# Rotary embedding moved from VectorE to GpSimd, in place in SBUF, with ScalarE copying whole heads out of PSUM

## The chip, the cores and the metric

The kernel runs on one core of one Trainium2 chip. The core has five engines that work side by side, each through its own list of instructions in order: TensorE (PE in the profile, with PEld for its weight loads), VectorE (DVE), ScalarE (ACT), GpSimd (POOL) and SyncE (SP), which issues most DMA transfers. The metric is the device time of one execution in microseconds; less is better. Runs of the kernel before took 1145.68, 1145.86 and 1147.49 us, the median is 1145.86 us.

## The reference: what is computed

The program is a trunk of two layers on 512 tokens of width 1024, each a token mixer and a squared-ReLU MLP with a layer norm behind each. The first mixer is sparse attention, and only that one uses the rotary embedding:

```python
def partial_rotary(t, cos, sin):
    half = cos.shape[-1]                       # 8; a head has 64 columns
    t1 = t[..., :half]; t2 = t[..., half:2 * half]
    return jnp.concatenate([t1 * c - t2 * s, t2 * c + t1 * s, t[..., 2 * half:]], axis=-1)

def dsa_mixer(x, cos, sin, w_in, w_o):
    q, k, v, iq, ik, iw = jnp.split(x @ w_in, A_SPLITS, axis=-1)
    q, k, iq, ik = (partial_rotary(z, cos, sin) for z in (q, k, iq, ik))
    # an indexer (iq, ik, iw) scores each causal key, the best 128 are kept,
    # softmax attention of 16 query heads over 4 key heads on the kept keys
```

Only the first 16 of a head's 64 columns are rotated; the other 48 pass through.

## The kernel before

Every matrix product is done in three passes (`mm3`, lines 197 to 199): both operands are split into a high part (`w_hi`, `XT` plane 0) and a low part (`w_lo`, `XT` plane 1). ScalarE casts the high part of a weight panel (L141), VectorE subtracts for the low part (L142). For the tokens `to_xt` transposes a tile of 128 tokens on TensorE (L242); ScalarE casts the high part of the result into `XT` (L244), VectorE subtracts the low part (L245). `XT` is what all products of the layer read, so a tile of tokens can start when its `XT` is there. `natural` computes one tile of 128 tokens times up to 512 columns into a PSUM bank `ps`, of which there are three.

Attention goes through five column panels of the input projection: 264 and 320 columns for the indexer (`iq`, `ik`), 512 for keys and values, twice 512 for the queries. In the first panel the tokens' tiles come in the order 1, 2, 3, 0, and `to_xt` of the next tile is done in the middle of a tile. Behind each tile stands `rotated` (19 tiles in all: 8 of 8 heads, 3 of 5, 7 of 4, 1 of one head), and behind that `stack_q` or `stack_k`: ScalarE casts the rotated tile `nat` into `hl` (L577) or `dup` (L595), VectorE subtracts for the low half (L578, L596; for `dup` ScalarE casts once more, L597), and one or two tiles later TensorE transposes it (L585, L605) and ScalarE copies the result away (L586, L607).

Meanwhile VectorE does other work. `index_scores` has TensorE compute scores (L631, L632, two PSUM banks `qk`), ScalarE apply relu (L634) and VectorE add them up (L636, L638). `top_k` then takes the 128 best of each row in rounds of MAX8 and MATCH_REPLACE8 (L679, L680), 16 rounds for each of three blocks, all on VectorE. Then the logits (L702, L703, again in `qk`), whose row extreme VectorE takes (L704), ScalarE's Exp (L708, L710), transposes (L717) and the product with the values.

GpSimd does nothing in attention. It first works in the MLP behind it, on weight combinations (L163 to L171), and later in the gated linear attention of layer two (L935, L1107).

A scheduler fixes the order of each engine's instructions when the program is built, from its own estimates and from the priorities of the code's order; on the chip each engine goes through its list in that order, and waits where an operand isn't ready.

Of the kernel before, what the change touches and what calls it, by code (L numbers as in the profile page):

```python
# [20 lines left out]
OP = mybir.AluOpType  # L21
# [84 lines left out]
class Trunk:  # L106
# [450 lines left out]
    def rotated(self, src, t, h):  # L557

        nc = self.nc
        src = src.rearrange("p (h d) -> p h d", d=64)  # L560
        dst = self.rt.tile([P, self.rt_h, 64], F32, name="nat")[:, :h, :]
        c = self.cos[:, t, None, None, :].to_broadcast([P, h, 2, 8])
        s = self.sin[:, :, t].rearrange("p two e -> p () two e").to_broadcast([P, h, 2, 8])
        x2 = src[:, :, 0:16].rearrange("p h (two e) -> p h two e", two=2)
        nc.scalar.copy(dst[:, :, 16:64], src[:, :, 16:64])
        a = self.rt.tile([P, self.rt_h, 2, 8], F32, name="rot_c")
        b = self.rt.tile([P, self.rt_h, 2, 8], F32, name="rot_s")
        nc.vector.tensor_tensor(a[:, :h], x2, c, op=OP.mult)
        nc.vector.tensor_tensor(b[:, :h], x2[:, :, ::-1, :], s, op=OP.mult)
        nc.vector.tensor_add(dst[:, :, 0:16].rearrange("p h (two e) -> p h two e", two=2), a[:, :h], b[:, :h])  # L570
        return dst

    def stack_q(self, nat, h, dst):
# [663 lines left out]
```

## Time and profile before

| | us |
|---|---|
| runs | 1145.68, 1145.86, 1147.49 |
| median | 1145.86 |
| profiled execution, its own time | 1145.4 |
| its span, first to last instruction | 1143.6 |
| busy: TensorE, VectorE, ScalarE, GpSimd | 1126.0, 883.2, 563.7, 212.9 |
| stretch with `rotated` in it | 12 to 135 |

The span lies inside the execution's time, 1.8 us less. Busy time of TensorE includes the modelled end of pipelined matmuls, so that small waits don't show in it; the idle time by stretch and the list of waits do.

### The profile page before, as it was taken

Reading aid. Unit: us, or ns where it says so; the run is one execution under the profiler, and the core shown is the slowest. Engines: PE = TensorE matmul, PEld = TensorE weight load, DVE = VectorE, ACT = ScalarE, POOL = GpSimd, SP = SyncE. Lnnn points to the kernel's source line nnn. Section 1 sums busy time; section 2 is a strip of 40 time slices with the busy share of each in tenths; the row PEclk is TensorE's granted clock in tenths of the full one; section 3 lists DMA queues with packets and bytes.
Section 4 is the critical chain, followed back from the end, with each engine's and each line's share of the span. In section 5 each row is a group of like instructions: output and inputs, shape, how many; then the busy total and the mean of one; then the engine's idle time right before and its main releaser. Section 6 shows DMA issues by size and latency. Waiting matters only on the chain. (4 is left out here: it accounts for less than half of the span.)

```text
span 1143.6 us, 16057 instructions
## 1 busy us (share of the span) xinstructions
PE 1126.0 (98%) x6039; PEld 943.5 (82%) x6039; DVE 883.2 (77%) x1592; ACT 563.7 (49%) x973; POOL 212.9 (19%) x136
## 2 busy tenths in 40 slices
PE   9999999999999999999999999999999999999997
PEld 7887888888888888888797887888988888888875
DVE  7899997687976786786885387567696876786787
ACT  6655786543544444353356476435344444343342
POOL 0000000002123213203301255110042123213221
PEclk9999999999999999999999999999999999999999
DMA  7322130521421431441432232052222421431321
GB/s 252 98 74 75 37 112 1 154 88 38 147 84 64 148 112 47 137 142 55 112 109 77 63 112 90 23 148 74 83 91 86 148 92 56 147 117 52 127 74 74
DMA packets 58198, 109.12 MB, mean 95 GB/s; under 512 B 5205, under 2 KB 10841, under 8 KB 58121
## 3 DMA queue, kind: packets, MB, share of 16 engines
q1 hardware_dynamic: 56968, 103.91, 28.7%
q0 software_dynamic: 1152, 4.19, 1.3%
q8 instruction: 47, 0.77, 0.3%
q14 instruction: 31, 0.25, 0.1%
HBM read 105.99 MB, written 2.10 MB: 95 GB/s over the span
## 5 line engine op out<-in xcount | busy, mean ns | idle before, releaser
L142 DVE TENSOR_TENSOR w_lo<-raw,w_hi 128x1024 fp32r<-128x1024 f32 (+4 forms) x220 | 288.9, 1331 | 29.1 <-ACT w_hi L141 26.7
L141 ACT CAST w_hi<-raw 128x1024 fp32r<-128x1024 f32 (+4 forms) x220 | 223.6, 1024 | 120.6 <-PE ps L199 45.8
L197 PE MATMUL ps<-XT,w_hi 128*128 128x512 f32 (+1 forms) x640 | 236.0, 369 | 0.0
L198 PE MATMUL ps<-XT,w_hi 128*128 128x512 f32 (+1 forms) x640 | 235.5, 368 | 0.0
L199 PE MATMUL ps<-XT,w_lo 128*128 128x512 f32 (+1 forms) x640 | 235.5, 368 | 0.0
L197 PE MATMUL ps<-w_hi,XT 128*128 128x512 f32 (+5 forms) x440 | 163.7, 372 | 0.8 <-ACT w_hi L141 0.8
L198 PE MATMUL ps<-w_lo,XT 128*128 128x512 f32 (+5 forms) x440 | 160.9, 366 | 0.6 <-DVE w_lo L142 0.6
L199 PE MATMUL ps<-w_hi,XT 128*128 128x512 f32 (+5 forms) x440 | 160.3, 365 | 0.0
L198 PEld LDWEIGHTS ps<-XT,w_hi 128*128 128x128 f32 x640 | 120.7, 189 | 20.2 <-issue 0.4
L197 PEld LDWEIGHTS ps<-XT,w_hi 128*128 128x128 f32 x640 | 120.6, 189 | 20.2 <-issue 0.2
L199 PEld LDWEIGHTS ps<-XT,w_lo 128*128 128x128 f32 x640 | 120.6, 188 | 20.1 <-issue 0.2
L163 POOL TENSOR_TENSOR raw<-raw 128x1024 f32<-128x1024 f32 x14 | 34.2, 2441 | 385.4 <-DVE w_lo L142 385.4
L197 PE MATMUL ps<-w_hi,form 128*128 128x512 f32 x260 | 102.2, 393 | 0.7 <-DVE big L419 0.7
L198 PE MATMUL ps<-w_lo,form 128*128 128x512 f32 x260 | 101.4, 390 | 0.0
L199 PE MATMUL ps<-w_hi,form 128*128 128x512 f32 x260 | 101.4, 390 | 0.0
L197 PEld LDWEIGHTS ps<-w_hi,XT 128*128 128x128 f32 x440 | 82.8, 188 | 12.0 <-ACT w_hi L141 1.0
L198 PEld LDWEIGHTS ps<-w_lo,XT 128*128 128x128 f32 x440 | 82.8, 188 | 11.1 <-DVE w_lo L142 1.0
L199 PEld LDWEIGHTS ps<-w_hi,XT 128*128 128x128 f32 x440 | 82.8, 188 | 10.9
L142 DVE TENSOR_TENSOR w_lo<-t,w_hi 128x1024 fp32r<-128x1024 f32 x14 | 30.3, 2164 | 72.7 <-ACT w_hi L141 72.7
L371 DVE TENSOR_TENSOR h<-h 128x512 f32<-128x512 f32 (+1 forms) x72 | 43.7, 624 | 44.2 <-ACT h L370 44.2
L370 ACT ACTIVATE h<-ps 128x512 f32<-128x512 f32 (+1 forms) x72 | 38.7, 546 | 61.5 <-PE ps L199 54.5
L141 ACT CAST w_hi<-t 128x1024 fp32r<-128x1024 f32 x14 | 14.7, 1049 | 105.3 <-POOL t L165 105.3
(248 smaller groups left out, 1950.4 us busy)
## 6 DMA issues: line engine op xcount, KB each, us to landing
raw<-in_mlp_w_up_dram SPq DMA_DIRECT2D x64, 512.0 KB, 4.4
raw<-in_mlp_w_down_dram SPq DMA_DIRECT2D x64, 512.0 KB, 4.4
raw<-in_b_w_in_dram SPq DMA_DIRECT2D x16, 512.0 KB, 4.9
raw<-in_a_w_in_dram SPq DMA_DIRECT2D x12, 512.0 KB, 4.6
big<-in_x_dram SPq DMA_DIRECT2D x8, 512.0 KB, 4.0
raw<-in_a_w_o_dram SPq DMA_DIRECT2D x8, 512.0 KB, 4.0
raw<-in_b_w_o_dram SPq DMA_DIRECT2D x8, 512.0 KB, 4.7
raw<-in_b_w_in_dram SPq DMA_DIRECT2D x8, 346.0 KB, 3.9
```

What stands on the lines that cost most here:

```text
L141: self.nc.scalar.copy(hi, src)
L142: self.nc.vector.tensor_sub(lo, src, hi.bitcast(F32))
L163: sub(t1, b12, b11)
L197: mmul(out, lhs[0], rhs[0], start=first, stop=False, skip_group_check=more)
L198: mmul(out, lhs[0], rhs[1], start=False, stop=False, skip_group_check=more)
L199: mmul(out, lhs[1], rhs[0], start=False, stop=last, skip_group_check=more)
L370: nc.scalar.activation(h, ps[:, :step], AF.Relu)
L371: nc.vector.tensor_mul(h, h, h)
```

## The change

`rotated` copies all 64 columns of each head out of the bank, not 48, and the three instructions that rotate the first 16 columns run on GpSimd in place of VectorE. They read the copy in SBUF, where they read the bank before, and the last writes over the 16 columns it was made from. So they now start after the copy, and the bank is released by the copy alone.

```diff
-        x2 = src[:, :, 0:16].rearrange("p h (two e) -> p h two e", two=2)
-        nc.scalar.copy(dst[:, :, 16:64], src[:, :, 16:64])
+        x2 = dst[:, :, 0:16].rearrange("p h (two e) -> p h two e", two=2)
+        nc.scalar.copy(dst, src)
         a = self.rt.tile([P, self.rt_h, 2, 8], F32, name="rot_c")
         b = self.rt.tile([P, self.rt_h, 2, 8], F32, name="rot_s")
-        nc.vector.tensor_tensor(a[:, :h], x2, c, op=OP.mult)
-        nc.vector.tensor_tensor(b[:, :h], x2[:, :, ::-1, :], s, op=OP.mult)
-        nc.vector.tensor_add(dst[:, :, 0:16].rearrange("p h (two e) -> p h two e", two=2), a[:, :h], b[:, :h])
+        nc.gpsimd.tensor_tensor(a[:, :h], x2, c, op=OP.mult)
+        nc.gpsimd.tensor_tensor(b[:, :h], x2[:, :, ::-1, :], s, op=OP.mult)
+        nc.gpsimd.tensor_tensor(x2, a[:, :h], b[:, :h], op=OP.add)
         return dst
```

The scheduler then orders attention anew; behind attention the lists are the same but for one ISA instruction of GpSimd, which stood ahead of its first subtraction (L163) and now stands ahead of the first rotation (L568), as GpSimd's first instruction of the kernel's own.

ScalarE in the first panel, from the copy of the first tile on (`nat` the rotated tile, `XT` the transposed tokens of the next). Before:

```order
L565 COPY nat<-ps 128x4x48
L577 CAST hl<-nat 128x3x64
L595 CAST dup<-nat 128x128
L244 CAST XT<-tps 128x4x128
L597 CAST dup<-dup 128x64
L244 CAST XT<-tps 128x4x128
L141 CAST w_hi<-raw 128x2x320 x2
L565 COPY nat<-ps 128x4x48
L244 CAST XT<-tps 128x4x128
```

Now:

```order
L565 COPY nat<-ps 128x256
L577 CAST hl<-nat 128x3x64
L595 CAST dup<-nat 128x128
L597 CAST dup<-dup 128x64
L244 CAST XT<-tps 128x4x128 x2
L141 CAST w_hi<-raw 128x2x320 x2
L565 COPY nat<-ps 128x256
L577 CAST hl<-nat 128x3x64
L595 CAST dup<-nat 128x128
L597 CAST dup<-dup 128x64
L244 CAST XT<-tps 128x4x128 x2
```

The last cast of `dup`, which needs VectorE's subtraction on the rotated tile, has moved ahead of the `XT` copies. With the second tile it is the same: `hl`, both casts of `dup`, then both copies to `XT`, where before one `XT` copy came first.

ScalarE at the first logits, in the query panels (`big` holds the transposed queries, `pr` the logits). Before:

```order
L565 COPY nat<-ps 128x8x48
L586 CAST big<-tps 128x512 x2
L708 ACT_TABLE_LOAD
L708 ACTIVATE pr<-pr,mx 128x128
L577 CAST hl<-nat 128x8x64
L708 ACTIVATE pr<-pr,mx 128x128 x4
```

Now:

```order
L565 COPY nat<-ps 128x512
L586 CAST big<-tps 128x512 x2
L577 CAST hl<-nat 128x8x64
L708 ACT_TABLE_LOAD
L708 ACTIVATE pr<-pr,mx 128x128 x5
L720 COPY pT<-tps 128x512
```

The `hl` cast has moved ahead of the load of the Exp table and of the first exponential. On VectorE the subtraction of this `hl` stood behind five L704 and now stands behind two. At the index scores of block 2 the `dup` cast of the first key tile has moved in the same way, from behind the first two relu instructions to ahead of them.

VectorE in the first half of the query panel, around the subtraction for the third tile's `hl` (`m` the eight greatest values of a round of top-k, `sc` the scores). Before:

```order
L679 MAX m_1311<-sc_218 128x8
L680 MATCH_REPLACE sc_218<-m_1311,sc_218 128x384
L142 TENSOR_TENSOR w_lo<-raw,w_hi 128x1024 x2
L578 TENSOR_TENSOR hl<-nat,hl 128x8x64
L679 MAX m_1314<-sc_218 128x8
L568 TENSOR_TENSOR rot_c<-ps,cos 128x128
L569 TENSOR_TENSOR rot_s<-ps,sin 128x128
```

Now:

```order
L679 MAX m_1317<-sc_218 128x8
L679 MAX m_1602<-sc_219 128x8
L680 MATCH_REPLACE sc_218<-m_1317,sc_218 128x384
L578 TENSOR_TENSOR hl<-nat,hl 128x8x64
L682 TENSOR_SCALAR sc_218<-sc_218 128x384
L142 TENSOR_TENSOR w_lo<-raw,w_hi 128x1024
L680 MATCH_REPLACE sc_219<-m_1602,sc_219 128x512
L142 TENSOR_TENSOR w_lo<-raw,w_hi 128x1024 x2
L679 MAX m_1605<-sc_219 128x8
```

The subtraction has moved ahead of the two `w_lo`. Of the 96 top-k instructions 82 now stand ahead of the first L704, 73 before; nine stand between it and the 33rd L704 in both.

## Rows read from the trace of the kernel before

**Rows 1.** The page of the profiled execution: its span, and part 1, busy time, share of the span and instructions of each engine.

```profile
span 1143.6 us, 16057 instructions
...
PE 1126.0 (98%) x6039; PEld 943.5 (82%) x6039; DVE 883.2 (77%) x1592; ACT 563.7 (49%) x973; POOL 212.9 (19%) x136
```

**Rows 2.** Busy time by stretch (from, to and length in us; then busy us and instructions of TensorE, its weight loads, VectorE, ScalarE and GpSimd, the granted clock of TensorE as a share of full speed, the share of DMA and its GB/s). The stretches are the first two panels and the start of the third, the key and value panel with the index scores, the first half of the query panel, the first logits, the second half of the query panel and the logits of block 1, the logits of blocks 1 and 2.

```profile
12.00:45.00 33.00, 33.00 (x239) 31.11 (x239) 25.18 (x64) 23.19 (x57) 0.00 (x0) 1.00 0.62 202
...
45.00:90.00 45.00, 44.97 (x229) 35.88 (x228) 44.11 (x127) 26.98 (x53) 0.00 (x0) 1.00 0.15 48
...
90.00:105.00 15.00, 14.23 (x73) 11.65 (x72) 14.81 (x35) 8.69 (x13) 0.00 (x0) 1.00 0.44 137
...
105.00:120.00 15.00, 14.14 (x93) 11.36 (x91) 14.86 (x62) 10.37 (x23) 0.00 (x0) 1.00 0.02 5
...
120.00:150.00 30.00, 29.86 (x214) 26.56 (x212) 26.40 (x85) 22.43 (x46) 0.00 (x0) 1.00 0.23 71
...
150.00:165.00 15.00, 14.54 (x97) 12.18 (x96) 14.63 (x41) 13.68 (x39) 0.00 (x0) 1.00 0.23 71
```

**Rows 3.** Waits from 12 to 165 us: who waited for whom; us in total, times, the longest. The rows are of TensorE (PE) and its weight loads (PEld).

```profile
PE tps L585 <- ACT w_hi L141: 0.8, 1, 0.8
...
PE qk L702 <- DVE mx L704: 0.6, 2, 0.4
...
PEld qk L702 <- DVE mx L704: 2.6, 6, 0.8
...
PEld tps L717 <- DVE XT L245: 0.6, 1, 0.6
```

**Rows 4.** The views of the tiles `nat` and `rot_s` over the whole span: line, engine, operation, how often; shortest, median and longest duration in ns; first and last start; the sizes.

```profile
L565 ACT COPY nat<-ps x19: 212/360/482, 12.6 to 132.4; 128x384 f32<-128x384 f32 x8, 128x192 f32<-128x192 f32 x7, 128x240 f32<-128x240 f32 x3, 128x48 f32<-128x48 f32 x1
...
L570 DVE TENSOR_TENSOR nat<-rot_c,rot_s x19: 174/241/286, 13.4 to 133.7; 128x128 f32<-128x128 f32 x8, 128x64 f32<-128x64 f32 x7, 128x80 f32<-128x80 f32 x3, 128x16 f32<-128x16 f32 x1
...
L569 DVE TENSOR_TENSOR rot_s<-ps,sin x19: 166/230/281, 13.2 to 133.1; 128x128 f32<-128x128 f32 x8, 128x64 f32<-128x64 f32 x7, 128x80 f32<-128x80 f32 x3, 128x16 f32<-128x16 f32 x1
```

**Rows 5.** The timeline in the gated linear attention, where GpSimd subtracts (start, duration, engine, line, operation, names and sizes, in brackets idle time before and what ended it): a copy on ScalarE and the two GpSimd instructions behind it.

```profile
650.66 0.45 ACT L1096 COPY big<-ps 128x346 f32<-128x346 f32 x1 [1.92 <-PE ps L199]
...
651.26 0.61 POOL L935 TENSOR_TENSOR Q<-gb 128x256 f32<-128x256 f32 x1 [3.19 <-ACT big L1096]
...
651.84 1.04 POOL L935 TENSOR_TENSOR E<-gb 128x512 f32<-128x512 f32 x1
```

**Rows 6.** The timeline of GpSimd and VectorE where GpSimd first computes, in the first MLP, and the view of line 389 over the whole span (shortest, median, longest ns of its 14 instructions).

```profile
214.09 0.53 POOL L326 DMA_DIRECT2D lngb<-in_ln_mlp_b_dram  x1
...
270.95 2.72 POOL L163 TENSOR_TENSOR raw<-raw 128x1024 f32<-128x1024 f32 x1 [56.33 <-DVE w_lo L142]
...
271.44 2.77 DVE L389 TENSOR_TENSOR big<-big,h 128x512 f32<-128x512 f32 x1
...
L389 DVE TENSOR_TENSOR big<-big,h x14: 673/675/2774, 271.4 to 1066.2; 128x512 f32<-128x512 f32 x14
```

**Rows 7.** The timeline of the first panel, ScalarE, then VectorE, then TensorE. The TensorE rows are the first matmul of the third and of the fourth tile.

```profile
12.61 0.32 ACT L565 COPY nat<-ps 128x192 f32<-128x192 f32 x1 [0.33 <-PE ps L199]
...
13.72 0.35 ACT L577 CAST hl<-nat 128x192 fp32r<-128x192 f32 x1 [0.79 <-DVE nat L570]
...
14.52 0.59 ACT L244 CAST XT<-tps 128x512 fp32r<-128x512 f32 x1 [0.25 <-PE tps L242]
...
16.88 0.33 ACT L565 COPY nat<-ps 128x192 f32<-128x192 f32 x1
...
18.28 0.59 ACT L244 CAST XT<-tps 128x512 fp32r<-128x512 f32 x1 [1.07 <-PE tps L242]
...
16.40 1.56 DVE L142 TENSOR_TENSOR w_lo<-raw,w_hi 128x640 fp32r<-128x640 f32 x2
...
18.90 0.69 DVE L245 TENSOR_TENSOR XT<-tps,XT 128x512 fp32r<-128x512 f32 x1 [0.42 <-ACT XT L244]
...
16.20 0.28 PE L197 MATMUL ps<-w_hi,XT 128*128 128x264 f32 x1
...
20.19 0.27 PE L197 MATMUL ps<-w_hi,XT 128*128 128x64 f32 x1
```

**Rows 8.** The timeline of ScalarE at the first index scores of block 2.

```profile
45.10 0.87 ACT L634 ACTIVATE r<-qk 128x384 f32<-128x384 f32 x2 [0.54 <-PE qk L632]
...
45.86 0.62 ACT L595 CAST dup<-nat 128x512 fp32r<-128x512 f32 x1
```

**Rows 9.** The timeline of VectorE ahead of the transposes of the third query tile.

```profile
91.85 0.56 DVE L679 MAX8 m<-sc 128x8 f32<-128x384 f32 x1
...
92.98 2.35 DVE L142 TENSOR_TENSOR w_lo<-raw,w_hi 128x1024 fp32r<-128x1024 f32 x2
...
95.25 0.69 DVE L578 TENSOR_TENSOR hl<-nat,hl 128x512 fp32r<-128x512 f32 x1
```

**Rows 10.** The timeline of ScalarE at the first logits.

```profile
108.01 0.48 ACT L565 COPY nat<-ps 128x384 f32<-128x384 f32 x1 [3.61 <-PE ps L199]
...
109.49 1.28 ACT L708 ACT_TABLE_LOAD   x1
...
110.78 0.40 ACT L708 ACTIVATE pr<-pr,mx 128x128 f32<-128x128 f32 x1
```

## The prediction, made before the changed kernel had run

> **What bounds the kernel now.** I read the page first [rows 1]: TensorE counts as busy for 98% of the span, VectorE for 77%, GpSimd for 19%. A share over the whole span says little about an edit that touches 19 tiles in one layer, so I went to the stretch in which `rotated` runs, 12 to 135 us, and to what follows it in attention, up to 165 us. The table by stretch [rows 2] shows two regimes. From 12 to 45 us TensorE has no idle time and VectorE has slack (25.2 of 33 us). From 45 to 120 us VectorE is full (44.1 of 45, 14.8 of 15, 14.9 of 15 us), because the top-k instructions fill every hole, and still TensorE idles only 0.03 + 0.77 + 0.86 us there, 0.14 us in the next 30 and 0.46 us in the 15 after. So a full VectorE is not the bound: it works off a queue that TensorE mostly doesn't wait for. What TensorE and its weight loads do wait for from 12 to 165 us is in [rows 3]: 0.8 us before the transposes of `hl` (L585), 0.6 us of matmul and 2.6 us of weight-load waits on the reduce of the logits (L704), 0.6 us on the `XT` subtraction. A weight-load wait is partly hidden behind the matmul before it, so it is an upper bound of what it costs. The granted clock is at its upper level in every stretch [rows 2], so the clock is no part of the case. The profiled execution took 1145.4 us, 0.46 us under the median of the three runs, 1145.86; I sum against 1145.4 and add the 0.46 at the end.
>
> **What VectorE gives up.** 57 instructions, three for each of 19 tiles, of 0.23 to 0.24 us in the median [rows 4], some 13.5 us of durations; they overlap their neighbours by about a quarter, so about 10 us of its time. None of it is TensorE time by itself. It pays only where a wait of [rows 3] ends earlier.
>
> **What GpSimd takes on.** The same 57 instructions, which no row shows on GpSimd in these sizes. Its nearest rows are two undisturbed subtractions in SBUF with a stretched operand, 0.61 us for 256 and 1.04 us for 512 elements per partition [rows 5]: 0.0017 us per element and 0.18 us fixed, so 0.29 us for 64 and 0.40 us for 128 elements. The lower bound is the fixed part, 0.18 us, the upper one 0.61 us, which is the larger row itself; I take the line. The start after ScalarE's copy costs about 0.15 us (a copy that ends at 651.11, GpSimd at 651.26 [rows 5]). From the end of the copy to the end of the addition that makes 0.15 + 3 x 0.29 + 0.1 = 1.1 us for four heads and 1.5 us for eight. Before, with four heads and VectorE free, it was 0.8 us from copy to `hl` [rows 7]; in the full stretch VectorE needs longer than that anyway, since its rotation stands behind top-k instructions.
>
> **What ScalarE takes on.** A quarter or a third more elements in 19 copies of 0.36 us [rows 4], at most 0.1 us each; ScalarE is busy for 105 of these 153 us [rows 2], so I put it at nothing apart from the places below. The costly thing is not the copy: `hl` and `dup` are ScalarE casts that wait for the rotation, everything behind them on ScalarE waits too, and the order has moved them forward.
>
> **Loss 1, the first panel.** ScalarE now does the second `dup` cast ahead of both `XT` copies (the first place shown in the section on the change). Tile three starts at 16.20 us on `XT` halves whose copy began at 14.52 [rows 7]. Now `hl` comes 0.4 us later and the third cast stands in front: the copy begins at about 15.2, VectorE's half (0.69 us [rows 7]) ends at about 16.5, and TensorE needs it 0.24 us after 16.20: 0.2 us lost (0 to 0.6). The next hand-over is worse. The copy of 16.88 slips to about 17.4; GpSimd could start at 17.95, but VectorE's two `w_lo` subtractions (1.56 us from 16.40 [rows 7], now from about 17.1) read SBUF twice. With 1.1 us of rotation and 1.0 us of `hl`, `dup`, the subtraction for `dup` and its cast, the `XT` copy begins at 20.0 to 20.6 instead of 18.28, and its second half is there at 21.3 to 21.9; the matmuls that stood at 20.19 need it at about 20.6. I take 1.0 us (0.6 to 1.6). Nothing behind it gives it back, since TensorE has no idle time in these 33 us.
>
> **Loss 2, the index scores.** `dup` moves from behind the second relu (45.86, the relus at 45.10) to ahead of both [rows 8], and waits for a rotation that can't end before 45.2. The relus come 0.7 us later; two banks of logits cover some of it. I take 0.5 us (0 to 1.3).
>
> **Loss 3, the first logits.** `hl` moves ahead of the load of the Exp table (the second place). The copy is at 108.01, the table at 109.49, the first exponential at 110.78 [rows 10]. Now `hl` can start at 110.1 and ends at 110.7, the table takes 1.28 us, the first exponential begins at 112.0: 1.2 us later. On VectorE `hl` stands behind the second L704 and holds the third until 111.4. TensorE's new order has three more matmuls of 0.23 us ahead of the first L717, which cover some 0.7 us. I take 0.5 us (0 to 1.2).
>
> **Gain 1.** The 0.77 us at 95.2 us: the transposes wait for an `hl` subtraction that ran at 95.25, behind two `w_lo` of 2.35 us together [rows 9]. In the new order it stands ahead of both (the third place). I take all, 0.8 us.
>
> **Gain 2.** VectorE reaches the first L704 without a rotation and with nine top-k instructions fewer outstanding, but the order still mixes nine of them with the next 32 L704, as before. Of 0.6 us idle and 2.6 us of weight-load waits [rows 3] I take 0.7 us (0 to 2.6).
>
> **Gain 3.** Top-k ends some ten microseconds of VectorE work earlier and both `w_lo` for the output projection leave the stretch after 150 us, while one `w_hi` of 1.05 us enters it. Of the 0.14 + 0.46 us idle and the 0.6 us behind `XT` [rows 2, 3] I take 0.5 us (0 to 1.2).
>
> **Sum.** Losses 0.2 + 1.0 + 0.5 + 0.5 = 2.2 us, gains 0.8 + 0.7 + 0.5 = 2.0 us: +0.2 us, 1145.6 for a profiled execution, 1146.0 for the median of runs. With all lower losses and upper gains it is 0.6 - 4.6 = -4.0 us, with the reverse 4.7 - 0.8 = +3.9 us.
>
> **Who blocks whom.** Where GpSimd ran a subtraction of 2.72 us, a VectorE instruction with two SBUF inputs that takes 0.675 us lasted 2.77 us [rows 6]: one of the two waits for the whole of the other. [...] If every VectorE instruction held GpSimd, it would be rival B.
>
> **Rivals.** A, faster: VectorE is the hidden bound from 90 to 165 us. For it speaks that it is full there and that all of [rows 3] but one names VectorE or what follows it. Against it: the same density of top-k between logits. It needs gains 2 and 3 near their ends and losses near the lower ones; about -3.4 us, 1142.5. B, slower, by one mechanism: GpSimd and VectorE exclude each other whatever the VectorE instruction. Then a GpSimd instruction stands behind the rest of a top-k instruction (0.56 us in the middle size [rows 9]) each time, so a rotation of 1.5 us becomes up to 3.2 us, and VectorE is held in turn, up to 57 x 0.3 to 0.4 us, more than the 10 us it gave up: gains 2 and 3 go, loss 2 becomes 1.3 and loss 3 2.2 us, 0.2 + 1.0 + 1.3 + 2.2 - 0.8 = +3.9 us, 1149.8. For it speaks how complete the blocking of [rows 6] is, against it that those rows are all of two SBUF inputs. It decides from about 0.18 us of VectorE held per GpSimd instruction, where the 10 us are used up. C, slower: an ISA instruction now stands ahead of the first rotation (it stood ahead of L163). If it is a code load that lasts beyond 12.9 us, the first `hl` and with it the `XT` copies wait, microsecond for microsecond; 15 us too long would give 1161. The trace can't price it: between the last DMA issue at 214.09 and the first subtraction at 270.95 GpSimd waited for data anyway [rows 6], so it lies between 0 and 56 us, and since that first subtraction isn't late I take the low end. [...]
>
> **Chances.** Near-cancellation 0.51, with a range of its own of 1143.7 to 1148.2; A 0.22, B 0.21, C 0.04; 0.02 for what I don't see. A run can tell about 0.2%, 2.3 us, from no change. The middle case spills a little over both bounds: faster 0.24, the same 0.50, slower 0.26. The range takes in the ends of the sum, 1142.0 to 1150.0.
>
> **What would show it.** In the changed profile the GpSimd rotations at 0.3 to 0.4 us each; a first-panel wait of about 1 us on `XT` at 20 us; no wait before the transposes at 95 us; the Exp table about 1 us later after the copy; L702 still waiting on L704. Wrong would be rotations of over 0.6 us, VectorE's MAX8 longer beside them, or a GpSimd that starts late.

## The result: 1.3% slower, and the profile after

The changed kernel ran in 1158.18, 1159.82, 1163.35 and 1165.86 us, median 1161.59; the kernel before beside it in 1145.8. The ratio is 1.0133, 95% interval 1.0113 to 1.0152. The profiled execution is the fastest of the four; its span is 1156.2 us, 12.6 us more than before. The page's first lines, against [rows 1]:

```profile
span 1156.2 us, 16080 instructions
...
PE 1131.0 (98%) x6039; PEld 948.5 (82%) x6039; DVE 878.0 (76%) x1535; ACT 565.8 (49%) x973; POOL 239.3 (21%) x193
```

VectorE gave up 5 us of busy time and GpSimd took on 26. Busy shares can't tell where 12.6 us went. The start of ScalarE's copy out of the bank, tile by tile, can, since TensorE's product ends just ahead of it:

| copy (L565) | before, us | after, us | later by |
|---|---|---|---|
| 1st, first panel | 12.61 | 13.26 | 0.65 |
| 5th, second panel | 27.49 | 33.29 | 5.80 |
| 7th, ahead of the index scores of block 1 | 36.31 | 42.14 | 5.83 |
| 8th, third panel | 43.58 | 52.00 | 8.43 |
| 13th, second query tile | 82.35 | 92.72 | 10.38 |
| 16th, first logits follow | 101.83 | 111.27 | 9.44 |
| 18th | 126.19 | 139.09 | 12.90 |
| end of the mixer, first L370 | 252.62 | 265.26 | 12.64 |

The loss is made in four places, all in attention: 5.2 us in the first panel, 2.6 at the index scores of block 1, 2 in the key panel, 3.5 at the first logits; 0.9 is gained at 95 us. The 0.65 at the start isn't the change's: other kernels below with the same beginning stand between -0.2 and +0.8 there.

The table by stretch, with the stretches and columns of [rows 2]:

```profile
12.00:45.00 33.00, 29.86 (x203) 28.40 (x201) 15.76 (x27) 19.41 (x45) 8.15 (x21) 0.90 0.49 157
45.00:90.00 45.00, 42.66 (x213) 33.59 (x214) 41.55 (x105) 28.92 (x60) 6.22 (x15) 1.00 0.25 80
90.00:105.00 15.00, 15.00 (x78) 12.45 (x77) 14.40 (x35) 7.35 (x12) 2.69 (x6) 1.00 0.01 1
...
120.00:150.00 30.00, 26.58 (x168) 22.92 (x168) 26.81 (x91) 20.66 (x43) 3.06 (x6) 0.94 0.15 44
```

Read two columns. TensorE is idle for 3.1, 2.3 and 3.4 us in the first, second and last stretch, where before it was idle for 0.00, 0.03 and 0.14 us. (The first logits, which now begin at 118 us, lay before in the stretch from 105 to 120 us, with 0.86 us idle.) And the granted clock, third from the end, is 0.90 and 0.94 in the first and the last stretch, where it was 1.00. Cut finer, with the same columns, after:

```profile
24.00:31.00 7.00, 7.00 (x36) 7.00 (x36) 4.49 (x6) 4.87 (x11) 0.62 (x3) 0.53 0.59 179
...
120.00:127.00 7.00, 4.09 (x19) 3.39 (x19) 6.79 (x27) 3.95 (x9) 0.00 (x0) 0.76 0.00 0
```

The first of these stretches before:

```profile
24.00:31.00 7.00, 7.00 (x52) 6.99 (x51) 4.07 (x11) 3.73 (x12) 0.00 (x0) 1.00 0.89 296
```

From 24 to 31 us TensorE never pauses, and yet does 36 matmuls where the kernel before does 52: the granted clock is 0.71 in the first of these microseconds and 0.50 in the other six. That costs 7 x 0.47 = 3.3 us; from 120 us on it is 7 x 0.24 = 1.7 us. TensorE's waits from 12 to 165 us, against [rows 3]:

```profile
PE qk L702 <- DVE mx L704: 3.5, 2, 3.3
PE qk L631 <- ACT r L634: 1.9, 3, 1.3
PE tps L585 <- DVE XT L245: 1.5, 1, 1.5
PE tps L605 <- ACT dup L595: 1.1, 1, 1.1
PE qk L631 <- ACT iqT L586: 0.8, 1, 0.8
```

The wait of [rows 3] at 95 us is gone; these five are new or longer. So the profiled execution lost some 5 us to the clock and the rest to waits. The other runs had mean clocks of 0.992, 0.988 and 0.985, the profiled one 0.993: what they lost beyond it goes with the clock.

**Where each wait comes from.** The first panel, by timelines of GpSimd, ScalarE and TensorE:

```profile
18.48 0.88 POOL L568 TENSOR_TENSOR rot_c<-nat,cos 128x64 f32<-128x64 f32 x1 [3.77 <-ACT nat L565]
...
20.99 0.24 ACT L597 CAST dup<-dup 128x64 fp32r<-128x64 f32 x1 [0.36 <-DVE dup L596]
21.14 1.07 ACT L244 CAST XT<-tps 128x512 fp32r<-128x512 f32 x2
...
22.50 0.45 PE L585 MATMUL tps<-ident_r,hl 128*128 128x128 f32 x3 [1.53 <-DVE XT L245]
```

The `XT` casts stood at 18.28 [rows 7] and 19.22 before; now they stand behind the last `dup` cast, and TensorE waits 1.53 us. It waits in the transposes of `hl`: they write to a bank `tps` that the `XT` subtraction has to read first. The index scores, on GpSimd and ScalarE:

```profile
42.63 1.45 POOL L568 TENSOR_TENSOR rot_c<-nat,cos 128x80 f32<-128x80 f32 x1 [3.74 <-ACT nat L565]
...
44.86 0.46 ACT L577 CAST hl<-nat 128x320 fp32r<-128x320 f32 x1 [1.66 <-POOL nat L570]
45.22 0.65 ACT L634 ACTIVATE r<-qk 128x256 f32<-128x256 f32 x2
```

A rotation lasts 1.45 us, four times its 0.36, beside two `w_lo` subtractions; `hl` waits for it, and the relus that TensorE needs stand behind `hl`. The first logits, TensorE and VectorE:

```profile
118.50 0.27 PE L702 MATMUL qk<-kT,big 128*128 128x128 f32 x1
...
121.97 0.68 DVE L680 MATCH_REPLACE8 sc<-m,sc 128x512 f32<-128x512 f32 x1
122.56 0.28 DVE L704 CUSTOM_DVE_ANT_0 pr<-qk,cft 128x128 f32<-128x128 f32 x1
122.91 0.33 PE L702 MATMUL qk<-kT,big 128*128 128x128 f32 x1 [3.26 <-DVE mx L704]
```

The first logits were there at 118.7, but L704 stands behind the last of 82 top-k instructions, and both `qk` banks are full.

### The profile page after: what moved, and what is told of

Read it like the earlier page. It is cut to its first block, busy times and chain, and to the rows that moved or that the text cites. A ratio compares the mean times of both kernels' runs of the same rounds, so it can differ in the third digit from the quotient of the medians.

```text
span 1156.2 us, 16080 instructions
## 1 busy us (share of the span) xinstructions
PE 1131.0 (98%) x6039; PEld 948.5 (82%) x6039; DVE 878.0 (76%) x1535; ACT 565.8 (49%) x973; POOL 239.3 (21%) x193
## 3 DMA queue, kind: packets, MB, share of 16 engines
q0 software_dynamic: 1152, 4.19, 1.3%
## 5 line engine op out<-in xcount | busy, mean ns | idle before, releaser
L163 POOL TENSOR_TENSOR raw<-raw 128x1024 f32<-128x1024 f32 x14 | 34.2, 2441 | 385.5 <-DVE w_lo L142 385.5
L197 PEld LDWEIGHTS ps<-w_hi,XT 128*128 128x128 f32 x440 | 84.0, 191 | 11.7 <-ACT w_hi L141 0.8
L199 PEld LDWEIGHTS ps<-w_hi,XT 128*128 128x128 f32 x440 | 84.2, 191 | 11.1
L370 ACT ACTIVATE h<-ps 128x512 f32<-128x512 f32 (+1 forms) x72 | 38.6, 545 | 59.8 <-PE ps L199 52.8
```

What stands on the lines that cost most here:

```text
L163: sub(t1, b12, b11)
L197: mmul(out, lhs[0], rhs[0], start=first, stop=False, skip_group_check=more)
L199: mmul(out, lhs[1], rhs[0], start=False, stop=last, skip_group_check=more)
L370: nc.scalar.activation(h, ps[:, :step], AF.Relu)
```

## The experiments

Medians are compared with runs of the kernel before on the same chip, 1146.9 to 1147.6 us in the median. Those runs go from 1145.2 us, at a mean clock of 0.998, to 1149.3 us, at 0.995: the clock varies by that much without any change.

**One group of tiles at a time.** `first_vec` and `only_first` split the change at the first panel. The edit calls the old `rotated` (here `rotated_v`) at the named places; one of the lines:

```diff
-                        nat = self.rotated(ps[:, 0:256], t, 4)
+                        nat = self.rotated_v(ps[:, 0:256], t, 4)
```

> The changed kernel, but the four tiles of the first panel rotate on VectorE out of the bank as before; the other 15 tiles stay on GpSimd, and every list behind the first panel stays as in the changed kernel. Theory 'wait, then clock': the wait of 1.7 us at 20.8 us (transposes of hl behind the late XT subtraction) and the half clock from 24.4 to 31 us that follows it go together; TensorE is 5 us earlier at the third panel and the median is 5 us under the changed kernel's 1161.6, so about 1156 to 1157. Rival 'ports' (GpSimd held by two-input VectorE instructions is what costs): only one of the eight held rotations lies in the first panel (0.88 in place of 0.32 us), so 0.6 us at most is gained. Rival 'clock falls by itself': the clock falls somewhere between 20 and 45 us anyway, gain under 2 us.

> The kernel before, but the four tiles of the first panel rotate on GpSimd as in the changed kernel; the 15 others stay on VectorE. 'Wait, then clock': the whole loss of the first panel returns, a wait of 1.5 to 1.7 us near 20.8 us and a stretch of some 6 us at half clock behind it, median 1145.8 + 5 = 1151 (1149 to 1152). 'Ports': 0.6 us at most, 1146.4. 'Clock falls by itself': within 2 us of before.

Measured: `first_vec` 1154.9 us, 6.7 under the changed kernel; `only_first` 1151.3, 4.3 over before (ratio 1.0034, 1.0020 to 1.0047). The stretch behind the first panel in both, columns as above:

```profile
24.00:31.00 7.00, 7.00 (x52) 6.98 (x51) 3.32 (x7) 3.59 (x11) 1.03 (x3) 1.00 0.90 300
```
```profile
24.00:32.00 8.00, 8.00 (x38) 8.00 (x38) 4.59 (x7) 4.81 (x11) 0.62 (x3) 0.50 0.59 172
```

With the rotations of four tiles the wait of 1.5 us and the half clock come and go together. "Ports" (one rotating instruction of 0.88 us in place of 0.32) and "clock falls by itself" are out as the account of this loss: they allow 0.6 and under 2 us.

The same with the other groups:

> The kernel before, but only the three tiles of five heads (second panel, ahead of the index scores of block 1) rotate on GpSimd. In the changed kernel TensorE lost about 3 us around them, in two waits of 0.8 and 1.3 us on the casts of iqT and on relu, with a rotation of the third tile that lasted 1.45 us in place of 0.36 beside the two-input subtraction w_lo. Theory 'waits': the order brings the waits back here, 1.5 to 3 us, median 1147.5 to 1150, and up to 3.4 us more in executions in which the clock falls behind them. Rival 'heritage' (the waits in the changed kernel came only from the panel before being late, so that weight loads and rotation met): nothing is lost, 1146 to 1147.

> The kernel before, but only the four tiles of keys (4 heads, third panel) rotate on GpSimd. 'Waits': the last rotation meets a w_lo subtraction and the dup transposes wait about 1.1 us, as at 82 us of the changed kernel; median 1146.5 to 1148.5, no clock fall from one wait of 1.1 us. 'Heritage': no such wait, 1145.5 to 1147.

> The kernel before, but only the eight query tiles (8 heads) rotate on GpSimd. The wait of 0.8 us at 95 us goes (-1.0 us in the changed kernel). At the first logits 78 top-k instructions stand ahead of the first L704 on VectorE (82 in the changed kernel, 73 before). 'Order': that is what made the 3.3 us wait, so here a wait of 1 to 2.5 us and in some executions the half clock behind it: median 1146.5 to 1150. Rival 'heritage' (the wait came from everything being 9 us late): no wait, the gain at 95 us stays, 1145.

| alone on GpSimd | median | over before | ratio, interval |
|---|---|---|---|
| first panel, 4 tiles | 1151.3 | 4.3 | 1.0034 (1.0020 to 1.0047) |
| five heads, 3 tiles | 1153.8 | 6.9 | 1.0053 (1.0034 to 1.0072) |
| keys, 4 tiles | 1148.9 | 2.0 | 1.0017 (1.0008 to 1.0026) |
| queries, 8 tiles | 1153.6 | 6.7 | 1.0063 (1.0048 to 1.0077) |

Each group loses by itself, so "heritage" is out. All three came out over what I expected, `only_kv` by 0.4 us, `only_idx` by as much even with the fall of the clock that I allowed for, `only_q` by 3.6. Their waits (of `only_idx`, then of `only_q`) and clock:

```profile
PE qk L631 <- ACT r L634: 1.4, 1, 1.4
PE qk L702 <- DVE mx L704: 1.2, 1, 1.2
...
105.00:130.00 25.00, 23.70 (x121) 21.23 (x120) 20.78 (x79) 14.32 (x31) 0.00 (x0) 0.73 0.02 7
```
```profile
PE qk L702 <- DVE mx L704: 3.9, 2, 3.4
...
110.00:120.00 10.00, 6.54 (x32) 5.64 (x32) 9.31 (x33) 6.04 (x13) 1.21 (x3) 0.66 0.00 1
```

In `only_idx` no rotation near the first logits is on GpSimd, and the order there still changed enough for a wait of 1.2 us; the clock then stayed down for most of 15 us. One of its six runs, at a mean clock of 0.996 in place of 0.989 to 0.991, took 1147.98 us, the others 1153.7 to 1155.1. The four losses sum to 20 us, more than the whole change's 15.8, since two of them pay for the same fall at the first logits.

**The copy without the engine.** `inplace_vec` has the three instructions on `nc.vector`, everything else as in the change.

> The changed kernel with the three rotating instructions on VectorE, still in place on ScalarE's copy of whole heads: it separates the copy and the dependence on it from the engine. 'Wait, then clock' with the engine's latency and the order that follows from it as the cause: a rotation of about 0.7 us behind the copy in place of 1.0 to 1.1, so waits in the first panel of 0 to 0.7 us, no clock fall, 1145 to 1149. Rival 'copy' (ScalarE's whole copy and the start behind it are the cause, whatever the engine): a wait over 1.2 us near 20 us and the clock fall return, over 1150.

Measured 1149.1 us, ratio 1.0022 (1.0013 to 1.0032). The copies of the first panel stand 0.1 to 0.2 us behind before, so the whole copy and the start behind it cost next to nothing there. The list changed at the first logits again: L702 waits 1.8 us on L704, and the clock from 110 to 120 us is 0.66. So 2 of the 16 us come without GpSimd, by the order; the rest comes with the move to GpSimd, by its longer rotation or by the order that goes with it, which this run doesn't separate.

**The wait filled.** `fill14` adds, ahead of the transposes that waited:

```diff
+    if upto == 3:
+        po = self.po.tile([P, 512], F32, name="po")
+        for _ in range(14):
+            self.nc.tensor.matmul(po[:, :256], self.ident_r, self.XT[:, 0, 0, P:3 * P], start=True, stop=True)
```

> The changed kernel with 14 additional matmuls of 256 columns, whose result nobody reads, directly ahead of the transposes of hl that waited at 20.8 us; 14 x 0.12 = 1.7 us, the length of that wait. Nothing else moves. 'Wait, then clock': the wait itself stays (TensorE does useless work in it), but the granted clock stays at 1.00 from 24 to 31 us, and the 3.3 us that the half clock cost are back: 1158.2 - 3.3 = 1155 for a profiled execution like the changed kernel's, median 3 to 4 us under 1161.6. If the clock falls for another reason than the idle time, the time stays or rises by up to 0.3 us.

```profile
20.00:24.00 4.00, 3.85 (x35) 3.66 (x33) 2.18 (x8) 2.24 (x8) 0.92 (x3) 1.00 0.54 207
24.00:31.00 7.00, 7.00 (x56) 6.99 (x56) 3.98 (x5) 5.92 (x15) 2.01 (x4) 1.00 0.53 175
```

At this place it did what "wait, then clock" says: clock 1.00, and the sixth copy stands 2.1 us later than the first one in place of 5.2, so 3.1 of the 3.3 us are back. The time didn't follow, 1160.8 us (ratio 1.0113, 1.0096 to 1.0130), 2 to 3 us over what I expected: in the profiled execution the clock fell at the next waits instead, to 0.67 from 40 to 45 us, where the changed kernel's profile shows none, and to 0.57 from 120 to 140 us. `fill_all` tried the same at all five waits:

> The changed kernel with matmuls of 256 columns that nobody reads in all its five longer waits: 14 at 20.8 us as before, 8 and 12 at the index scores of block 1 (42 and 44 us), 10 at the last dup transposes (81 us), 28 at the first logits (119 us), 0.12 us each. Theory: the changed kernel loses about 6 us in waits and the rest of its 15.7 us in the clock falls that follow them, whose number differs from run to run. Then the waits stay and the falls go: median 1149 to 1153 and runs within 3 us of each other, where the changed kernel ran from 1158 to 1166. If the falls have another cause, it stays over 1157.

It took 1168.2 us, and doesn't tell what I asked. The first four groups held the clock at 1.00 up to 125 us; the 28 matmuls at the logits moved the list, VectorE again reached L704 late, a wait of 3.1 us came behind them, and the clock from 125 to 145 us was 0.57.

**A wait put into the kernel before.** This takes everything else of the change away: the rotations stay on VectorE, and one transpose of TensorE reads a tile that GpSimd fills n times (5, 8, 11). Order constraints, left out here, hold TensorE's transposes of `hl` and `dup` and the fourth tile's product behind it.

```diff
+    if upto == 3:
+        gap = self.raw_gap
+        self.nc.gpsimd.tensor_copy(gap[:, :64], self.nat[:, 0, :])
+        for _ in range(n):
+            self.nc.gpsimd.memset(gap[:, :512], 0.0)
+        self.gate = self.nc.tensor.transpose(po[:, :P], gap[:, :P], self.ident)
```

> The kernel before, rotations on VectorE, with one added thing: at 20 us, where the changed kernel's TensorE waited, TensorE must first transpose a tile that GpSimd (idle otherwise) fills after the second tile's rotation with one copy and five fills of 512 columns. The length of the fill isn't in any row, the wait is read from the run; the shortest of three, expected 0.3 to 1 us. If the wait alone makes the clock fall, a short one costs its own length and no more: 1146.5 to 1148. If the falls in the changed kernel belong to something else that GpSimd's rotations bring, the same.

> The same with eight fills, expected wait 1.2 to 2.5 us, like the changed kernel's 1.7. 'The wait itself makes the clock fall': the granted clock goes to 0.50 some 2 us behind the end of the wait for about 6 us, and the median is the wait plus 3.3 us over before: 1150.5 to 1152.5. Rival (the falls of the changed kernel come from something else): the wait costs its own length, 1148 to 1149.5, clock 1.00 from 22 to 35 us.

> The same with eleven fills, expected wait 2 to 4 us. 'The wait itself': clock at 0.50 again, for as long as or longer than behind the shorter wait, median 1151 to 1155. Rival: the wait's own length, 1148 to 1150.5.

The fills took longer than I assumed, so even the shortest wait is as long as the changed kernel's. Waits and clock, of `dose5`, `dose8` and `dose11`:

```profile
PE po L1264 <- POOL gap L1262: 1.7, 1, 1.7
...
24.00:31.00 7.00, 7.00 (x35) 7.00 (x35) 4.49 (x8) 4.68 (x9) 0.00 (x0) 0.54 0.65 216
```
```profile
PE po L1264 <- POOL gap L1262: 3.4, 1, 3.4
...
26.00:33.00 7.00, 7.00 (x34) 7.00 (x34) 4.58 (x8) 4.58 (x9) 0.00 (x0) 0.51 0.64 204
```
```profile
PE po L1264 <- POOL gap L1262: 5.2, 1, 5.2
...
25.00:35.00 10.00, 9.88 (x47) 9.88 (x48) 4.58 (x8) 5.47 (x11) 0.06 (x1) 0.50 0.47 132
```

Medians 1152.0, 1155.0 and 1157.1, over before by 4.9, 7.9 and 9.9 us: 3.2, 4.5 and 4.7 more than the wait. In the profiles the copies behind this place stand 4.9, 6.7 and 9.9 us later than those ahead of it: the wait's own delay, 1.9, 3.6 and 5.3 us by the landmarks around it, and some 3.0, 3.1 and 4.6 us of half clock. The price doesn't grow with the wait in step: after the first two the clock is down for some 7 us, after the third for 10, as 7 x 0.46 = 3.2, 7 x 0.49 = 3.4 and 10 x 0.50 = 5 say too. The profiles of the two longer ones hold another fall at 690 us, which is no part of this. A fall at this place is also found in three of twelve profiles without such a wait (the table below), so that one case would show little. Here it is three of three, and the mean clock of all twelve runs is 0.992 to 0.995, where the 17 runs of the kernel before have 0.995 to 0.998. So a wait by itself, with every rotation on VectorE, brings the fall at this place.

**The order without the engine's move undone.** If the waits are the scheduler's lists, constraints on the lists should remove them with all rotations left on GpSimd. `a_xt` traces `stack_q` and `stack_k` of a tile behind the next `XT` casts, `a_pin6` holds the last rounds of top-k behind the second L704 (of each edit the lines that set the order):

```diff
+                        with tc.issue_after(self.cast.ins):
+                            while hold:
+                                hold.pop()()
```
```diff
+                        if b == NT - 1 and i >= 6: pin.enter_context(tc.issue_after(live["first"].ins))
```

> The changed kernel, all rotations on GpSimd as they were, but in the first panel ScalarE does both XT copies of the next tile ahead of the hl and dup casts of the tile before (an order constraint; TensorE's list stays as it is). Theory 'order': the 1.7 us wait at 20.8 us came from the place of those casts in ScalarE's list, not from GpSimd being slower than VectorE; the wait goes, the half clock behind it goes, and the median is near that of the kernel whose first panel rotates on VectorE, 1153 to 1157. Rival 'latency' (a rotation of 1.1 us on GpSimd is too late in any order): a wait of over 1 us at another instruction of the first panel, median over 1158.

> The changed kernel, but from its seventh round on the top-k of the last block is constrained behind the second L704 on VectorE, so that 76 top-k instructions stand ahead of the first L704 in place of 82 (73 in the kernel before); nothing ahead of it moves. Theory 'order': the wait of 3.3 us at 119 us came from those top-k instructions (six of 0.7 us are 4.2 us), and with it go the wait and the half clock behind it: 3 us for the wait and 2 to 6 us of clock, median 1152 to 1157. Rival 'VectorE is late anyway': the wait moves to a later L704 or the block behind, gain under 2 us.

> Both order constraints together, on the changed kernel. What stays are the waits at the index scores of block 1 (2.5 us), at the last dup transposes (1.2 us), and the gain of 1 us at 95 us. Theory 'order': 1146 + 2.5 + 1.2 - 1 = 1148.7 when the clock doesn't fall, up to 3.4 us more when it falls once, median 1148 to 1152. If the loss is not the order's, it stays over 1155.

> As the one with both constraints, and the hl cast of the third five-head tile is constrained behind the fourth relu of the index scores of block 1 on ScalarE, so that the relus don't wait for a rotation which a two-input VectorE instruction holds. Theory 'order': the wait of 1.3 us on relu goes, but in the new list a weight cast of 1.05 us stands ahead of the relus, which may bring back a part: 0.5 to 1.5 us under the kernel with both constraints. Rival: the rotation isn't what the relus waited for, and nothing changes.

`a_xt`: 1154.8 us, as good as the first panel on VectorE; the same stretch:

```profile
24.00:31.00 7.00, 7.00 (x53) 6.99 (x53) 3.83 (x6) 4.63 (x12) 1.80 (x6) 1.00 0.83 272
```

So GpSimd's slower rotation alone isn't what cost 5 us there: with the `XT` casts ahead of `hl` and `dup` the panel loses about 0.5 us in place of 5.2. Whether a quicker rotation would have saved the new order, no run shows. `a_pin6`: 1159.7, only 1.9 under the changed kernel, which the intervals don't separate, and over what I expected. Its wait on L704 and its clock there:

```profile
PE qk L705 <- DVE mx L707: 0.7, 2, 0.5
...
120.00:130.00 10.00, 8.49 (x60) 7.01 (x59) 8.58 (x38) 8.29 (x18) 1.33 (x3) 1.00 0.01 2
```

At its place the constraint did what "order" says: the longest wait went from 3.3 to 0.5 us, no fall of the clock follows, and between copies 16 and 18 TensorE loses 0.6 us in place of 3.5. Behind it 0.8 us are lost up to the end of the mixer, where the changed kernel gained 0.3. The rest of the gain was eaten in front, where the constraint changes nothing: in this execution the clock was 0.53 from 23 to 34 us (5.2 us lost) and 0.57 from 47 to 51, and copy 16 stands 12.1 us late, 9.4 in the changed kernel's profile. `a_both`: 1153.4, over the 1148 to 1152 expected, three of its six runs at 1152.0 to 1152.3, the others with the clock lower. `a_three`: 1155.9; its wait on relu went from 1.3 to 0.4 us, so that link of the chain is right, but VectorE then reached L704 late by 0.9 us and the clock fell behind it (0.66 from 115 to 130 us). The median is 2.5 us over `a_both`, within what the intervals allow. The constraint on top-k, from an earlier round on, in the kernel before:

> The kernel before, all rotations on VectorE, with the top-k of the last block held behind the second L704 from its fourth round on, so that 70 in place of 73 top-k instructions stand ahead of the first L704. If the place of top-k in VectorE's list is worth time in the kernel before too, its waits of 0.6 and 2.6 us on L704 shrink: 0.5 to 1.5 us faster, 1144.5 to 1146. Rival: VectorE idles ahead of the logits and the deferred rounds come back as waits at 140 to 150 us, as in the changed kernel with such a constraint: no gain or 1 to 2 us slower.

1150.6 us, ratio 1.0025 (1.0013 to 1.0036): slower. Its longest wait of matmuls on L704 is 0.4 us as before. A part of its loss can't be the constraint's: in the profile the clock is 0.66 from 23 to 28 us, ahead of all top-k. No version here beats the kernel before.

## Why the prediction was wrong, step by step

**The clock.** "The clock is no part of the case" is the step that failed. I took it from a profile in which no wait of TensorE is over 0.8 us, and didn't ask what the waits that I myself forecast would do to it. With the dose runs its price at the first panel is known: 3 to 5 us behind a wait of 1.5 us or more. At the first logits a fall cost from 1.7 us, in the changed kernel, up to 20 x 0.43 = 8.6 us, in `fill14`.

The clock is not all of it. The profiled execution lost 12.6 us where the sum has 0.2. Of the 12.4 us between them the clock is 5.0. Some 6 are waits that the sum lacks or has too small: 2.6 at the index scores of block 1, 1.5 in the key panel (2.0 measured, 0.5 forecast), 2.0 at the first logits. The shift at the start is 0.65. So without a fall it would still have been some 1153 us, over the range, and the median lies 3.4 us above that execution.

Over the 18 profiles (before, after, 16 experiments):

| place | wait of TensorE | clock fell in it or close behind |
|---|---|---|
| first panel | 1.5 us or more | 6 of 6 |
| first panel | none over 0.4 us | 3 of 12 |
| first logits | 0.9 us or more | 9 of 9 |
| first logits | 0.5 us or less | 0 of 9 |
| index scores of block 1 | 0.8 and 1.3 us | 3 of 7 |
| last `dup` transposes | 0.9 to 1.1 us | 0 of 7 |

Why a wait at one place always brings a fall and at another never is not settled; nor is why it fell three times in the first panel without one, and near 690 us in 10 of the 18, with and without the change.

**Loss 1, the first panel.** The waits were about right, and behind the `XT` casts as described: 0.2 and 1.0 us forecast, 0.2 and 1.5 measured. The 3.3 us of clock were missing.

**Loss 2, the index scores.** Forecast 0.5 us, with an end at 1.3, for block 2, where 0.4 were lost (copies 8 and 9 of the trace stand 8.43 and 8.85 us late). The 2.6 us were lost at block 1, which the sum doesn't have. I looked at the `dup` cast of block 2 and not at the `hl` cast of block 1, which had also come ahead of its relus, waiting for the rotation that `w_lo` held (1.3 us), nor at the three weight casts ahead of the `iqT` cast (0.8 us). The waits at the last `dup` transposes, 1.1 us, have the same cause (a rotation of 1.30 us beside `w_lo`) and weren't in the sum. I had priced the hold by `w_lo` once, in the first panel, and should have looked for every `w_lo` ahead of which a rotation now stood.

**Loss 3 and gain 2, the first logits.** Forecast -0.5 and +0.7, measured -3.5. The Exp table wasn't on the path: it was loaded by 121.5, and the first exponential waited for L704 until 122.9. "Nine top-k instructions fewer outstanding" was read with the wrong sign: it is nine more ahead of L704, and at about 0.75 us each they take longer than the 17 rotating instructions of the query tiles, 0.24 us each, that VectorE no longer does ahead of it. `a_pin6` shows that their place makes the wait. The count that I gave for what lies between the first and the 33rd L704 was wrong too: by the traces nine top-k instructions stand up to the 17th in both, and up to the 33rd it is 23 before and 14 now.

**Right.** Gain 1: 0.8 forecast, 0.9 measured. Gain 3: 0.5 forecast, 0.3 measured. GpSimd's instructions: 0.32 us for 64 elements and 0.46 for 128, forecast 0.29 and 0.40; they start 0.08 us behind the copy, forecast 0.15. The longer copies on ScalarE cost next to nothing in the first panel (`inplace_vec`). VectorE's share was not right: I put what it gives up at about 10 us, and its busy time fell by 5.2.

**Rivals.** A fell with gain 2. B fell: the views of L568 and of MAX8 after, then MAX8 before:

```profile
L568 POOL TENSOR_TENSOR rot_c<-nat,cos x19: 222/462/1452, 13.7 to 146.0; 128x128 f32<-128x128 f32 x8, 128x64 f32<-128x64 f32 x7, 128x80 f32<-128x80 f32 x3, 128x16 f32<-128x16 f32 x1
```
```profile
L679 DVE MAX8 m<-sc x48: 418/561/695, 51.8 to 138.7; 128x8 f32<-128x256 f32 x16, 128x8 f32<-128x384 f32 x16, 128x8 f32<-128x512 f32 x16
```
```profile
L679 DVE MAX8 m<-sc x48: 411/557/695, 44.0 to 145.3; 128x8 f32<-128x256 f32 x16, 128x8 f32<-128x384 f32 x16, 128x8 f32<-128x512 f32 x16
```

The median rotation of eight heads takes its 0.46 us in the midst of top-k, and MAX8 takes 561 ns in the median, 557 before. Seven of the 57 instructions lasted 0.77 to 1.45 us, each of them beside a `w_lo` subtraction with its two SBUF inputs; beside MAX8 and MATCH_REPLACE8 alone none was longer than elsewhere. At 62.23 us, in the midst of MAX8 (0.43 us) and MATCH_REPLACE8 (0.41), the three instructions for four heads took 0.32 us each, against 0.32 to 0.33 at 13.71 us, ahead of all top-k. That top-k holds no rotation was taken for granted in the sum; no row of before shows it. C fell too: the first rotation starts at 13.71, behind a copy that ends at 13.63. What the ISA instruction loads, if anything, is not shown; the trace has it at 0.8 us, 12.9 ahead of the first rotation. That C's example gave 1161 and the median is 1161.6 is chance.

## What to carry to other kernels

Where TensorE is the bound and runs without a pause, don't price a new wait of a microsecond or more at its length alone. Here one of 1.5 us or more in the first panel cost 3 to 5 us of half clock on top, each time; waits of about 1 us did so at some places and not at others. Carry that as a rival with a price of its own, and look at the granted clock of the stretch behind the wait in the profile of after. Moving work to an idle engine reorders the lists of the busy ones: read for every consumer of the moved result what now stands behind it in its own engine's list (here `XT` casts, relus, L704), because that can cost more than the moved instructions themselves, as it did here. If a list is at fault, one constraint on it tells so at once, but check what it pushes later.

## What the runs showed of the hardware

A wait of 1.7, 3.4 or 5.2 us at the same place was each time followed by 7 to 10 us at the lower clock, with a TensorE that was busy for 7.00 of 7, 7.00 of 7 and 9.88 of 10 us in them (clock 0.54, 0.51 and 0.50). Behind the waits of 1.7 and 3.4 us the fall begins 2.0 and 1.7 us after the wait has ended; behind that of 5.2 us TensorE came back at the lower clock already. With the first panel's wait filled by useless matmuls (`fill14`) no fall followed there, clock 1.00 from 20 to 31 us; it came at the next waits, of 0.8 and 1.4 us, with 0.67 from 40 to 45 us, where the changed kernel's profile, with waits of 0.8 and 1.3 us, has 1.00. Since a fall comes there in three of seven profiles, one case doesn't show that the filling moved it.
